# A hybrid retention and attention layer on one core: stores on another queue, loads in order, and late operands moved

## The chip, the cores and the metric

The kernel runs on one core of one Trainium2 chip. The metric is the device time of one execution in microseconds (us). TensorE does the matrix multiplications into PSUM (eight banks), VectorE (DVE in the profile) and ScalarE (ACT) the elementwise work, GpSimd (POOL) and SyncE (SP) issue transfers between the core's SBUF and HBM; ACT can issue them too.

## The reference

One layer over 512 tokens of 1024 channels, all in 32-bit floats:

```python
h = rms_norm(x, norm_mix)
rq, rk, rv, rg, cq, ckv, krope, gr, gm = split(h @ w_in)     # 4 retention heads, latents, two gates
ro = retention(rope(rq), rope(rk), rv)                       # heads of 256 and 512
ro = rms_norm(ro, ret_norm)
a_ret = (ro * silu(rg)) @ w_br
q, (k, v) = rms_norm(cq) @ w_uq, rms_norm(ckv) @ w_ukv       # 8 attention heads
a_mla = causal_attention(norm+rope(q), norm+rope(k), v) @ w_bm
x = x + (sigmoid(gr) * a_ret + sigmoid(gm) * a_mla) @ w_o
x = x + square(relu(rms_norm(x) @ w_up)) @ w_down
x = x + sigmoid(rms_norm(x) @ w_ple_gate) * (p @ w_ple)
```

## The kernel before

Everything is kept transposed, 128 channels by 512 tokens to a tile. Each 32-bit operand is split into a high part in TensorE's 32-bit format and the rest (`split`, lines 303 to 313), and each product is three multiplications (`mm3`). Weights come as chunks from one stream: `prepare` (lines 221 to 248) issues a chunk's load into one of 6 raw tiles (NRAW), `load_chunk` makes the high part on ACT and the rest on VectorE. The retention's v and gate and the MLP's second weight use a seven-product scheme on 2 by 2 blocks, in the order 1, 7, 2, 6, 5, 4, 3. There some weights are sums of blocks: SP loads one block and POOL adds another to it while loading (`accum_op`, line 227). Some operands are sums too: product 7 takes the difference of two token halves of the first four residual tiles, and products 6, 5 and 3 similar sums.

The work is written as a list of steps (`step(key, function, arguments)`), run in order by `run_steps`. A step with a key uses that chunk of weights; its loop prepares and converts chunks shortly ahead (AHEAD, PREP). Matrix multiplications keep the order in which they are written. The other engines' instructions are placed by a scheduler, which works with times of its own and can put an instruction in another place than it is written; `tc.keep_in_program_order` pins one behind the one written before it on its engine.

Tiles: `T(...)` takes one of NDYN = 45 tiles of the pool `dyn`, `K(...)` one of NKEEP = 16 of the pool `keep`. An instruction that needs a tile waits until one is free. The attention outputs (`mos`) hold all 16 keep tiles until the last product with `w_bm`.

The order of the stages, in which the change moves things:

- **Start.** Eight tiles of x (`x0` to `x7`) and eight chunks `a1` are loaded on SP; from them come the key/value latent (`pA`), then the query latent (`pcq`). `gn` (gains) is loaded from ACT, `cst` and `posi` from POOL.
- **Attention.** For each of 8 heads: `scores`, then other work while the softmax is made, `transposes` of the probabilities (`pt`), and in the next head's time `attend` (`mo`). `kq_head` projects two heads ahead; `pair_sums`, `pair_stats` (`st`, `hr`) and `head_factor` (`pbk`, `kf`) make the normalising factors of the next pair of heads, `rotary_stats` (`sqr`, from `sa`) those of four heads' rotary part. Between them stand fillers, `fill`: halves of the gate product `gm` and of head 0's `rq`, `rk` and the first `gr`, each 12 multiplications of 512 columns.
- **bm.** Eight products `branch_m`: each loads the gate that was put aside in HBM by `aside`, multiplies it by the product and puts it aside again (`am`). After each, `norm_x` loads one tile of x again (`xr`), scales it and splits it (`xn`). After all eight, `x_operands` makes the sums for products 7, 6, 5, 3 in keep tiles (`s70h` and so on).
- **Retention.** For each of 4 heads: `rq`, `rk`; for heads 0 and 2 the seven products `rv` of two heads; the branch products `br` of the head before; gate products `rg`, scores `rs`, `ret_attend` (`ro`), `ret_stats` (root `ro`, line 330), `ret_factor` (broadcast `pbo`, then four multiplications), `ret_gated` (gate, then the split `rog`). The branch outputs of head 0 are put aside, those of heads 1 and 2 added to them by POOL.
- **Gate, output, MLP, embedding.** Not touched by the diff.

The part of the list for the odd heads of attention:

```python
            if more:
                if h == 3:
                    step(None, rotary_stats, 1)
                step(None, pair_sums, p + 1)
                step(("v", p + 1), value_pair, p + 1)
                step(None, pair_stats, p + 1)
            else:
                fill(1)
            step(None, attend, h - 1)
            fill(1)
            step(None, transposes, h)
            if more:
                step(None, head_factor, h + 1)
                step(None, head_factor, h + 2)
            fill(1)
```

Of the kernel before, what the change touches and what calls it, by code (L numbers as in the profile page):

```python
# [151 lines left out]
def trunk_layer(ctx: ExitStack, tc: tile.TileContext, xT, pT, pos, gains, const, decay, wstream, outT):  # L152
# [68 lines left out]
    def prepare(key):  # L221

        if key[0] == "sw":
            _, blk, p, c = key

            def more(raw, kb, fb):
                nc.gpsimd.dma_start(raw, chunk(("w", blk, kb, fb, c)), accum_op=ALU.add)  # L227

            if p in (6, 4):
                return more(dw[blk, "t", c], *((0, 0) if p == 6 else (1, 0)))  # L230
            kb, fb = {1: (0, 0), 7: (0, 1), 2: (1, 0), 5: (0, 1), 3: (1, 1)}[p]
            nm = f"{blk[0]}{blk[1]}{p}{c}"
# [12 lines left out]
        nm = "_".join(str(x) for x in key)  # L245
        raw = wpool.tile([P, width], F32, tag="wraw", name="wr_" + nm, padded_shape=[P, 1024], bufs=NRAW)
        nc.sync.dma_start(raw, chunk(key))
        dw[key] = raw
# [23 lines left out]
    def run_steps():  # L272
        order = list(dict.fromkeys(k for k, _, _ in steps if k is not None))
        rank = {k: i for i, k in enumerate(order)}
        loaded = prepared = len(wt)
# [82 lines left out]
    nc.scalar.dma_start(gn, gains)  # L358
    posi = dyn.tile([P, S], I32, tag="t", name="posi")
    nc.gpsimd.dma_start(cst, const)  # L360
    nc.gpsimd.dma_start(posi, pos.partition_broadcast(P))
    xs, xg = [], []
    for k in range(8):
        t = T(f"x{k}")
        nc.sync.dma_start(t, xT[:, k])
# [335 lines left out]
    def x_operands():  # L701

        lo_, hi_ = slice(0, 256), slice(256, 512)
        for p, k0, cs in ((1, 0, lo_), (2, 4, lo_), (4, 4, hi_)):
            XS[p] = [(xn[k0 + k][0][:, cs], xn[k0 + k][1][:, cs]) for k in range(4)]

        def keep_split(p, c, t):
            hl = split(t, None, hi=K(f"s{p}{c}h", F32R), lo=K(f"s{p}{c}l", F32R))
            XS.setdefault(p, []).extend(cut(hl, kk * 256, 256) for kk in range(2))

        ts = [T(f"sx{c}") for c in range(2)]
        for p in (7, 6, 5, 3):
            for c in range(2):
                t = T(f"sy{c}") if p == 5 else ts[c]
                for kk in range(2):
                    k, o = 2 * c + kk, t[:, kk * 256:kk * 256 + 256]
                    if p == 7:
                        TT(o, xr[k][:, hi_], xr[k][:, lo_], op=ALU.subtract)
                    elif p == 6:
                        TT(o, xr[4 + k][:, hi_], o, op=ALU.subtract)  # L720
                    elif p == 5:
                        TT(o, xr[k][:, hi_], xr[4 + k][:, hi_], op=ALU.subtract)
                    else:
                        TT(o, xr[4 + k][:, lo_], o, op=ALU.subtract)
                keep_split(p, c, t)
# [96 lines left out]
    def ret_factor(h):  # L822
        r = R[h]["r"]
        R[h]["bc"] = bcast(B(f"pbo{h}"), lambda b: r[:, b:b + 1])
        for m in range(4):
            TT(R[h]["og"][m], R[h]["og"][m], R[h]["bc"], op=ALU.mult)

# [21 lines left out]
    def ret_gated(h):  # L849
        d = R[h]  # L850
        for m in range(4):
# [3 lines left out]
            d["rog"][m] = split(d["og"][m], f"rog{h}{m}")  # L855
# [270 lines left out]
    for h in range(MH):  # L1126
        p, more = h // 2, h + 2 < MH
        step(None, scores, h)
        if h % 2 == 0:
# [10 lines left out]
            if h == 2:  # L1140
                step(("qr", 1), query_rotary, 1)
            step(None, transposes, h)
            if h == 2:
                step(None, rotary_out, 1)
            fill(1)
        else:
            if more:
                if h == 3:
                    step(None, rotary_stats, 1)
                step(None, pair_sums, p + 1)  # L1150
                step(("v", p + 1), value_pair, p + 1)
                step(None, pair_stats, p + 1)
            else:
# [13 lines left out]
    fill(len(fillers))  # L1167
    step(None, mo_split, MH - 1)
    for n in range(8):
        step(("bm", n), branch_m, n)  # L1170
        step(None, norm_x, n)
    step(None, x_operands)
    for h in range(RH):
        for key in ("rq", "rk"):
            for n in range(2 if h else 0):
                step((key, h, n), ret_qk, h, key, n)
        left = [(("br", h - 1, k), branch_r, h - 1, k) for k in range(4 if h else 0)]
# [17 lines left out]
        step(None, ret_factor, h)  # L1195
# [3 lines left out]
    for n in range(EARLY, EARLY + 2):  # L1199
        step(("gr", n), gate_r, n)  # L1200
    for k in range(4):
# [113 lines left out]
```

## Time and profile before

| | |
|---|---|
| median of 3 runs | 1156.58 us (1153.46 to 1157.91) |
| profiled execution | 1155.4 us |
| its span | 1153.6 us |
| TensorE busy | 1110.3 us, 96% of the span |
| VectorE, ScalarE, GpSimd busy | 737.8, 537.0, 70.7 us |
| mean granted TensorE clock | 0.991 of full speed |
| moved by DMA | 173.33 MB, mean 150 GB/s |

A row of the profile's order of time reads: start and length in us from the span's start, engine (a q behind it: the engine's sequencer, which issues transfers), line of the kernel, operation, written tile <- read tiles, shape, count; in brackets the engine's idle time before it and what ended that. PE is TensorE's multiplication, PEld its weight load. A row of the chain of waits gives start, length and what ran. A row of the waits gives who waited <- for whom: total us, times, longest. Many rows have the line of a helper (172 for a multiplication, 265 to 269 for a weight's conversion, 308 to 312 for a split), so they are told apart by their tiles.

### The profile page before, as it was taken

The page shows a single profiled execution, that of the slowest core. Times are in us where ns is not written, and L with a number is a line of the kernel's source. Part 1 is how long each engine was busy: PE and PEld are TensorE (multiplying, and loading weights), DVE is VectorE, ACT ScalarE, POOL GpSimd, SP SyncE. Part 2 cuts the span into 40 slices and gives each one's busy share as a digit, 9 for nine tenths or more (in the row PEclk, how much of TensorE's full clock was granted, in tenths as well). Part 3 has the DMA queues.
Part 4 walks back from the last instruction along what each step waited for, and adds up shares of the span by engine and source line. Part 5 has one row for each costly group of instructions (what it writes and reads, how often), then busy time and mean ns, then how long its engine had stood idle before and what let it go on. Part 6 is the DMA issues. An engine that isn't in the chain of part 4 may idle for free.

```text
span 1153.6 us, 14652 instructions
## 1 busy us (share of the span) xinstructions
PE 1110.3 (96%) x5540; PEld 939.6 (81%) x5540; DVE 737.8 (64%) x1205; ACT 537.0 (47%) x762; POOL 70.7 (6%) x86
## 2 busy tenths in 40 slices
PE   6998989999699999999999999999999999999998
PEld 4887878888589788888989888888888888888877
DVE  5786666674775836745674765555567567568775
ACT  5555646553565344454534533433454344445542
POOL 0000000000110000121012000000100100101000
PEclk9998999999899999999999999999999999999999
DMA  6224121248785463598449443675756756747511
GB/s 224 76 79 131 55 76 62 74 157 248 178 224 138 137 186 119 131 208 239 132 130 194 146 182 109 192 243 168 151 163 196 155 159 179 169 143 192 155 36 73
DMA packets 59477, 173.33 MB, mean 150 GB/s; under 512 B 7088, under 2 KB 8368, under 8 KB 59152
## 3 DMA queue, kind: packets, MB, share of 16 engines
q1 hardware_dynamic: 47616, 134.24, 34.0%
q0 software_dynamic: 11648, 38.15, 19.1%
q8 instruction: 43, 0.70, 0.2%
q14 instruction: 26, 0.21, 0.1%
q10 hardware_dynamic: 144, 0.03, 0.0%
HBM read 155.61 MB, written 14.68 MB: 148 GB/s over the span
## 4 chain that ended last, share of the span: by engine, by line
PE 88%; DVE 5%; DMA 3%; ACT 2%; issue 2%; SPq 0%; POOL 0%; ACTq 0%; POOLq 0%; DVEq 0%
PE up L172 15%; PE dn L172 13%; PE br L172 8%; PE rv L172 5%; PE rg L172 5%; PE pg L172 4%; PE rq L172 4%; PE rk L172 4%; PE gr L172 4%; PE wo L172 3%; PE bm L172 3%; PE gm L172 3%; PE ro L172 3%; PE sc L172 2%; DMA wr_rg<-wstream 2%
## 5 line engine op out<-in xcount | busy, mean ns | idle before, releaser
L172 PE MATMUL dn<-wh_dn,cl 128*128 128x512 f32 x224 | 87.2, 389 | 0.0
L172 PE MATMUL dn<-wh_dn,ch 128*128 128x512 f32 x224 | 87.2, 389 | 0.0
L172 PE MATMUL dn<-wl_dn,ch 128*128 128x512 f32 x224 | 87.1, 389 | 0.0
L265 ACT ACTIVATE wh_dn<-wr_dn 128x1024 fp32r<-128x1024 f32 x32 | 34.0, 1062 | 75.5 <-PE up L172 54.3
L265 ACT ACTIVATE wh_up<-wr_up 128x1024 fp32r<-128x1024 f32 x32 | 34.0, 1061 | 57.7 <-PE up L172 29.3
L267 DVE TENSOR_TENSOR wl_dn<-wr_dn,wh_dn 128x1024 fp32r<-128x1024 f32 x32 | 39.1, 1221 | 27.4 <-ACT wh_dn L265 27.4
L267 DVE TENSOR_TENSOR wl_up<-wr_up,wh_up 128x1024 fp32r<-128x1024 f32 x32 | 39.1, 1223 | 18.5 <-ACT wh_up L265 18.1
L267 DVE TENSOR_TENSOR wl_rg<-wr_rg,wh_rg 128x1024 fp32r<-128x1024 f32 x20 | 24.5, 1225 | 40.5 <-ACT wh_rg L265 40.2
L172 PEld LDWEIGHTS dn<-wh_dn,ch 128*128 128x128 f32 x224 | 42.0, 188 | 8.8
L172 PEld LDWEIGHTS dn<-wh_dn,cl 128*128 128x128 f32 x224 | 42.0, 188 | 8.7
L172 PEld LDWEIGHTS dn<-wl_dn,ch 128*128 128x128 f32 x224 | 42.0, 188 | 8.6
L956 DVE SCALAR_TENSOR_TENSOR f<-up,bcx 128x512 f32<-128x512 f32 x32 | 20.6, 686 | 44.2 <-PE up L172 44.2
L265 ACT ACTIVATE wh_dn<-dr_dn 128x1024 fp32r<-128x1024 f32 x24 | 25.4, 1060 | 42.5 <-PE up L172 29.2
L267 DVE TENSOR_TENSOR wl_dn<-dr_dn,wh_dn 128x1024 fp32r<-128x1024 f32 x24 | 29.4, 1223 | 22.4 <-ACT wh_dn L265 22.4
L227 POOL DMA_DIRECT2D dr_dn<-wstream x24 | 21.7, 906 | 330.6 <-DVE rx L330 138.5
L265 ACT ACTIVATE wh_rg<-wr_rg 128x1024 fp32r<-128x1024 f32 x28 | 29.5, 1055 | 20.9 <-DMA wr_rg<-wstream 15.6
L265 ACT ACTIVATE wh_rv<-wr_rv 128x1024 fp32r<-128x1024 f32 x28 | 29.4, 1057 | 17.9 <-PE rv L172 6.3
L227 POOL DMA_DIRECT2D wr_rv<-wstream x16 | 13.8, 885 | 382.5 <-DMA wr_rv<-wstream 272.0
L863 ACT ACTIVATE rt<-br 128x512 f32<-128x512 f32 x24 | 14.3, 597 | 41.6 <-PE br L172 24.1
L1014 DVE TENSOR_TENSOR d<-d,dn 128x1024 f32<-128x1024 f32 x24 | 29.3, 1219 | 6.5 <-PE dn L172 6.5
L267 DVE TENSOR_TENSOR wl_br<-wr_br,wh_br 128x1024 fp32r<-128x1024 f32 x16 | 19.6, 1222 | 18.8 <-ACT wh_br L265 18.8
L265 ACT ACTIVATE wh_br<-wr_br 128x1024 fp32r<-128x1024 f32 x16 | 16.9, 1057 | 28.8 <-PE rk L172 17.8
(1889 smaller groups left out, 3620.8 us busy)
## 6 DMA issues: line engine op xcount, KB each, us to landing
wr_up<-wstream SPq DMA_DIRECT2D x32, 512.0 KB, 4.2
wr_dn<-wstream SPq DMA_DIRECT2D x32, 512.0 KB, 3.5
dr_dn<-wstream POOLq DMA_DIRECT2D x24, 512.0 KB, 8.4
wr_rv<-wstream SPq DMA_DIRECT2D x20, 512.0 KB, 4.5
wr_rg<-wstream SPq DMA_DIRECT2D x20, 512.0 KB, 5.2
wr_rv<-wstream POOLq DMA_DIRECT2D x16, 512.0 KB, 7.9
wr_rg<-wstream POOLq DMA_DIRECT2D x16, 512.0 KB, 6.2
wr_br<-wstream SPq DMA_DIRECT2D x16, 512.0 KB, 3.6
```

The source lines that it names most:

```text
L172: return tc.keep_in_program_order(nc.tensor.matmul(*a, **k))
L227: nc.gpsimd.dma_start(raw, chunk(("w", blk, kb, fb, c)), accum_op=ALU.add)
L265: ACT(hi, raw, AF.Copy, scale=sign)
L267: TT(lo, raw, hi.bitcast(F32), op=ALU.subtract)
L863: ACT(t, ps, AF.Copy)
L956: STT(u[:, i], ps[:, i], 0.0, V["bcx2"], op0=ALU.max, op1=ALU.mult)
L1014: TT(to, to, dps[p], op=ALU.add if sign > 0 else ALU.subtract)
```

## The change

- `aside` issues its 24 stores (8 `zm`, 8 `am`, 8 `ret`) from POOL and not from SP.
- Start: the loads of x0 to x7 go out from ACT in order, with `gn` behind x0; six chunks `a1` go out from SP in order, then `cst` and `posi`; the last two `a1` chunks keep that order too.
- `x_operands` becomes `x_operand(p)`, one step for each product. Product 7's operand is made after bm 2, its four parts in `dyn` tiles; the others after bm 7, as before in keep tiles. `norm_x` begins two tiles earlier, ahead of the last `mo_split`.
- `ret_factor` stands behind the next head's first `rq` product (for the last head, behind the first `gr` product), after the gating; it now makes the split too, the first two outputs of four in keep tiles.
- Attention: head 0's filler stands ahead of its transposes; for odd heads `attend` stands ahead of `rotary_stats` and `pair_stats`, and the last filler between transposes and head factors.

```diff
-        nc.sync.dma_start(raw, chunk(key))
+        tc.keep_in_program_order(nc.sync.dma_start(raw, chunk(key))) if key[0] == "a1" else nc.sync.dma_start(raw, chunk(key))
...
-        loaded = prepared = len(wt)
+        loaded, prepared = len(wt), len(dw)
...
         d = spill.tile([P, S], F32, tag=name, name=name + "d")
-        nc.sync.dma_start(d, t)
+        nc.gpsimd.dma_start(d, t)
...
-    nc.scalar.dma_start(gn, gains)
-    nc.gpsimd.dma_start(cst, const)
-    nc.gpsimd.dma_start(posi, pos.partition_broadcast(P))
     for k in range(8):
-        t = T(f"x{k}")
-        nc.sync.dma_start(t, xT[:, k])
-        xs.append(t)
-        if k < 3:
+        xs.append(T(f"x{k}"))
+        tc.keep_in_program_order(nc.scalar.dma_start(xs[k], xT[:, k]))
+        if k == 0:
+            tc.keep_in_program_order(nc.scalar.dma_start(gn, gains))
+        if k < 6:
             prepare(("a1", k))
-            load_chunk(("a1", k))
-            xg.append(split(t, f"xg{k}", g(G_MIX + k)))
+    tc.keep_in_program_order(nc.sync.dma_start(cst, const))
+    tc.keep_in_program_order(nc.sync.dma_start(posi, pos.partition_broadcast(P)))
+    for k in range(3):
+        load_chunk(("a1", k))
+        xg.append(split(xs[k], f"xg{k}", g(G_MIX + k)))
...
+            new = T if p == 7 else K
+            hl = split(t, None, hi=new(f"s{p}{c}h", F32R), lo=new(f"s{p}{c}l", F32R))
...
-            d["rog"][m] = split(d["og"][m], f"rog{h}{m}")
+    def ret_factor(h):
+        d, r = R[h], R[h]["r"]
+        bc = bcast(B(f"pbo{h}"), lambda b: r[:, b:b + 1])
+        for m in range(4):
+            TT(d["og"][m], d["og"][m], bc, op=ALU.mult)
+            new = K if m < 2 else T
+            d["rog"][m] = split(d["og"][m], None, hi=new(f"rog{h}{m}h", F32R), lo=new(f"rog{h}{m}l", F32R))
...
+            if h == 0:
+                fill(1)
             step(None, transposes, h)
...
-            fill(1)
+            if h:
+                fill(1)
         else:
+            if more:
+                step(None, pair_sums, p + 1)
+                step(("v", p + 1), value_pair, p + 1)
+            else:
+                fill(1)
+            step(None, attend, h - 1)
             if more:
                 if h == 3:
                     step(None, rotary_stats, 1)
-                step(None, pair_sums, p + 1)
-                step(("v", p + 1), value_pair, p + 1)
                 step(None, pair_stats, p + 1)
-            else:
-                fill(1)
-            step(None, attend, h - 1)
             fill(1)
             step(None, transposes, h)
+            fill(1)
             if more:
                 step(None, head_factor, h + 1)
                 step(None, head_factor, h + 2)
-            fill(1)
...
     fill(len(fillers))
+    step(None, norm_x, 0)
+    step(None, norm_x, 1)
     step(None, mo_split, MH - 1)
     for n in range(8):
         step(("bm", n), branch_m, n)
-        step(None, norm_x, n)
-    step(None, x_operands)
+        if n < 2:
+            step(None, norm_x, 2 + n)
+        elif n == 2:
+            step(None, x_operand, 7)
+        elif n < 7:
+            step(None, norm_x, n + 1)
+    for p in (1, 2, 6, 5, 4, 3):
+        step(None, x_operand, p)
...
                 step((key, h, n), ret_qk, h, key, n)
+                if (key, n) == ("rq", 0):
+                    step(None, ret_factor, h - 1)
...
-        step(None, ret_factor, h)
         step(None, ret_gated, h)
...
         step(("gr", n), gate_r, n)
+        if n == EARLY:
+            step(None, ret_factor, RH - 1)
```

More of the change, by code (lines that the diff above doesn't have):

```diff
@@ L699, in norm_x, with x_operand @@
         xn.append(split(t, f"xn{k}"))
-    def x_operands():
+    def x_operand(p):
         lo_, hi_ = slice(0, 256), slice(256, 512)
-        for p, k0, cs in ((1, 0, lo_), (2, 4, lo_), (4, 4, hi_)):
+        if p in (1, 2, 4):
+            k0, cs = {1: (0, lo_), 2: (4, lo_), 4: (4, hi_)}[p]
             XS[p] = [(xn[k0 + k][0][:, cs], xn[k0 + k][1][:, cs]) for k in range(4)]
[L707 to L722, printed above, removed]
-                    else:
-                        TT(o, xr[4 + k][:, lo_], o, op=ALU.subtract)
-                keep_split(p, c, t)
+            return
+        if p == 7:
+            V["sx"] = [T(f"sx{c}") for c in range(2)]
+        XS[p] = []
+        for c in range(2):
+            t = T(f"sy{c}") if p == 5 else V["sx"][c]
+            for kk in range(2):
+                k, o = 2 * c + kk, t[:, kk * 256:kk * 256 + 256]
+                if p == 7:
+                    TT(o, xr[k][:, hi_], xr[k][:, lo_], op=ALU.subtract)
+                elif p == 6:
+                    TT(o, xr[4 + k][:, hi_], o, op=ALU.subtract)
+                elif p == 5:
+                    TT(o, xr[k][:, hi_], xr[4 + k][:, hi_], op=ALU.subtract)
+                else:
+                    TT(o, xr[4 + k][:, lo_], o, op=ALU.subtract)
+            new = T if p == 7 else K
+            hl = split(t, None, hi=new(f"s{p}{c}h", F32R), lo=new(f"s{p}{c}l", F32R))
+            XS[p].extend(cut(hl, kk * 256, 256) for kk in range(2))
     CHAIN = {1: "a", 6: "a", 5: "a", 3: "a", 7: "c", 4: "c", 2: "b"}
@@ L820, in ret_stats @@
         R[h]["r"], _ = mean_rsqrt(f"ro{h}", st, RV)
[L822 to L826, printed above, removed]
     rgps = {}
```

2 lines of the change are left out of this document (1 added, 1 removed).

## The prediction

> **What bounds the kernel now.** I read the shares of busy time first, then the chain that ended last, then TensorE's own waits, and last the instructions in order of time around the largest of those waits.
>
> ```profile
> span 1153.6 us, 14652 instructions
> PE 1110.3 (96%) x5540; PEld 939.6 (81%) x5540; DVE 737.8 (64%) x1205; ACT 537.0 (47%) x762; POOL 70.7 (6%) x86
> ...
> PE 88%; DVE 5%; DMA 3%; ACT 2%; issue 2%; SPq 0%; POOL 0%; ACTq 0%; POOLq 0%; DVEq 0%
> ```
>
> TensorE is busy for 96% of the span and holds 88% of the chain. Nothing in the diff adds or removes a matrix multiplication, so what can be won is in TensorE's idle time, 1153.6 - 1110.3 = 43 us, and in the multiplications that run slowly after an idle stretch. The waits of TensorE, longest first (total, times, longest):
>
> ```profile
> PE rv L172 <- DVE s70l L309: 8.4, 1, 8.4
> PE pbo L172 <- DVE ro L330: 6.6, 4, 1.7
> PE pA L172 <- ACT xg0h L311: 4.8, 1, 4.8
> PE pbk L172 <- DVE hr L599: 3.8, 3, 1.5
> PE pt0a L172 <- ACT q2h L311: 3.5, 1, 3.5
> PE pA L172 <- ACT xg1h L311: 2.9, 1, 2.9
> PE sqr L172 <- DVE sa L557: 2.1, 1, 2.1
> PE st L172 <- ACT sums L584: 1.3, 1, 1.3
> ```
>
> Each row is a place that the diff moves: product 7's operand (s70l), the head factor of the retention (pbo), the start (pA), the key factors (pbk), the first transposes (pt0a), the statistics (sqr, st). No row names a weight's DMA: the queues wait a great deal, but TensorE does not wait for them. So the work on the queues is worth little by itself, and I price the four places in turn. All prices are set against the profiled execution's own 1155.4 us, which is 1.2 us under the median of the runs, 1156.58.
>
> **Part 1: the start.** Order of time, the first 31 us:
>
> ```profile
> 0.73 0.41 ACTq L358 DMA_DIRECT2D gn<-gains  x1
> 1.18 1.28 ACT L265 ACT_TABLE_LOAD   x1 [1.18 <-PEq L1308]
> 1.64 3.67 SPq L247 DMA_DIRECT2D wr_a<-wstream  x6
> 4.07 0.72 ACT L311 ACTIVATE xg0h<-x,gn 128x512 fp32r<-128x512 f32 x1 [0.36 <-DMA x<-xT]
> 4.84 0.80 PE L172 MATMUL pA<-xg0h,wl_a 128*128 128x512 f32 x1 [4.84 <-ACT xg0h L311]
> 5.36 0.59 SPq L365 DMA_DIRECT2D x<-xT  x1
> 11.36 0.72 ACT L311 ACTIVATE xg1h<-x,gn 128x512 fp32r<-128x512 f32 x1 [1.17 <-DMA x<-xT]
> 12.13 0.66 PE L172 MATMUL pA<-xg1h,wl_a 128*128 128x512 f32 x1 [2.90 <-ACT xg1h L311]
> 28.45 0.39 PE L172 MATMUL pA<-xg7h,wl_a 128*128 128x512 f32 x1
> 30.49 0.39 PE L172 MATMUL pcq<-xg0h,wl_cq 128*128 128x512 f32 x1
> ```
>
> Six weight loads stand on SP ahead of x1, which is issued at 5.36 and is only there at 11.36. A step is nine multiplications, 30.49 - 28.45 = 2.04 us at pace, so eight steps are 16.3 us; they take 30.49 - 4.84 = 25.65 us, 9.3 us too many. The change puts x0 to x7 in order on ACT's queue beside the weights on SP, so x1 lands soon after x0, and the wait of 2.9 us and the second slow stretch behind it go. It costs something too: nine DMA issues (gn and eight x) now stand on ACT ahead of its first conversion. By the SP row an issue in a row takes 3.67/6 = 0.61 us, so ACT is free at about 0.73 + 9 x 0.61 = 6.2 us; the table load of 1.28 us then follows them in place of running beside the first load, and a weight conversion (three quarters of xg0h's columns, about 0.5) and xg0h (0.72) bring the first multiplication to about 8.7 us, 3.9 later than now. After it only one slow stretch of about 2.6 us over the pace is left: 8.7 + 16.3 + 2.6 = 27.6 against 30.49, a gain of 2.9; I take 3. Ends: if the two queues' issues hold each other up to twice 0.61 us, ACT is free 5.5 us later and 2.6 us are lost; if the issues take 0.41 like gn's, 1.8 us more are won, 4.7 in all.
>
> The Trainium skill (DMA: Bandwidth & Descriptors, section Issuing engines are not separate DMA queues) says that DMAs started from several engines run on the same DMA engines, and that a second queue saves only issue time. By that alone the start would gain nothing, and the sum below would be 1135. The rows above say that it was the order on one queue that kept x1 back, so I keep the 3 us.
>
> Moving cst and posi behind the weights on SP I cost at nothing: TensorE first reads cst behind the latent products. The mask's two copies on ACT read it too; if they stand early in ACT's order, they wait for it there, which I leave inside the ends.
>
> **Part 2: attention.** The first transposes, and the chain of small VectorE steps behind one pair's factors:
>
> ```profile
> 104.30 0.82 DVE L641 TENSOR_SCALAR p<-p,rs 128x384 f32<-128x384 f32 x2
> 105.26 1.09 PE L172 MATMUL pt0a<-cst,p 128*128 128x128 f32 x4 [3.50 <-ACT q2h L311]
> 108.28 0.63 PE L172 MATMUL gm<-xg0h,wh_gm 128*128 128x512 f32 x1
> 121.28 0.17 DVE L595 TENSOR_TENSOR ha<-st,f 128x16 f32<-128x16 f32 x1
> 127.38 0.17 DVE L599 TENSOR_TENSOR hr<-hr,f 128x16 f32<-128x16 f32 x1
> ```
>
> TensorE stands still for 3.5 us until the softmax rows are scaled (104.30 + 0.82), then takes 0.63 for a multiplication that takes 0.39 in the rows of part 1. A filler of 12 multiplications (12 x 0.227 = 2.7 us) now stands in that gap: 2.7 of the 3.5 us go, and with a gap of 0.8 us no slow stretch should follow (some nine multiplications, each about 0.2 late, near 2.0). Behind it, scores of head 1 come 2.7 us sooner against transposes and projections whose PSUM banks are not yet emptied; I set 0.5 against it. Gain 4.2.
>
> For the odd heads, attend moves ahead of the pair's statistics and a filler moves between the transposes and the factor's broadcast. The VectorE chain takes 127.38 - 121.28 + 0.17 = 6.3 us. After the change two fillers and ten transposes (2.7 + 1.4 + 2.7 = 6.8, with four transposes at the 0.62 of part 4's row) lie between the statistics and the broadcast, so of the three pbk waits (3.8) I leave 0.5. The waits on sa (2.1) and on sums (1.3) have attend's 12 multiplications ahead of them now, some 2 us, and go. Gain 3.3 + 2.1 + 1.3 = 6.7, less 0.4 for what else may come late: 6.3. Part 2: 10.5, ends 6 (the banks cost 2 to 3, half of pbk stays) and 13.
>
> **Part 3: product 7's operand.** The last residual tile is asked for late, and the operand's sums stand behind it:
>
> ```profile
> 296.87 0.43 SPq L696 DMA_DIRECT2D xr<-xT  x1
> 304.69 0.75 DVE L697 SCALAR_TENSOR_TENSOR xr<-xr,gn,rbc 128x512 f32<-128x512 f32 x1 [1.94 <-DMA xr<-xT]
> 307.09 1.43 DVE L718 TENSOR_TENSOR sx<-xr 128x256 f32<-128x256 f32 x4
> 309.51 0.80 PE L172 MATMUL rv<-wh_rv,s70l 128*128 128x512 f32 x1 [8.41 <-DVE s70l L309]
> 310.10 0.63 PE L172 MATMUL rv<-wl_rv,s70h 128*128 128x512 f32 x1
> 310.53 0.63 PE L172 MATMUL rv<-wh_rv,s70h 128*128 128x512 f32 x1
> ```
>
> ```profile
> 301.00:306.00 5.00, 0.10 (x1) 0.00 (x0) 2.00 (x3) 2.10 (x3) 1.36 (x2) 0.99 1.07 235
> ```
>
> The sums need only xr0 to xr3, but VectorE did them behind xr7, which came at 304.69; and their results lay in the 16 keep tiles, all held by the attention outputs until the last bm product. With tiles of their own, and sums made when bm 2 is issued, they are ready more than 20 us before TensorE gets there. The 8.4 us go, and so does the slow stretch: seven steps of 0.43 in place of 0.23, with the first at 0.59, together 1.6. That is 10.0.
>
> What is late next: the weights. The last row is the stretch in which TensorE stood still (columns: length, busy time of PE, PEld, DVE, ACT, POOL, then granted clock, DMA share, GB/s): the DMA engines were full (1.07) while TensorE waited, so part of the stall hid transfers that the products after it need. Taken away, 10 us less lie between the bm products and product 3. For it: two xr loads are moved ahead of the bm products, SP no longer waits for each gated product before it issues the next load, and VectorE has made product 7's sums already. I set 3 us against it, ends 0 and 8. Part 3: 7.
>
> Stores: the 24 store issues move from SP to POOL. On SP nothing that TensorE waits for stood behind them (no weight row above), so nothing is gained there directly. On POOL they stand between the accumulating weight loads. One of POOL's accumulating stores, of head 2's branch:
>
> ```profile
> 602.59 0.87 POOL L867 DMA_DIRECT2D ret0d<-rt  x1 [1.71 <-ACT rt L863]
> ```
>
> That is the mix already: it takes 0.87 us and waits on ACT, and TensorE's waits have no row for the gate products behind it. A store that waits on its producer delays an accumulating load by one branch step at most. Cost 0.5, ends 0 and 3.
>
> The Trainium skill (DMA: Bandwidth & Descriptors, section SWDGE vs HWDGE vs iDMA) gives plain copies to SP and ACT, since GpSimd writes its descriptors in software and can be locked out by VectorE. By that rule the stores would be dearer; here 0.87 us of issue on an engine busy 6% of the span is no bound, so I leave the sum.
>
> **Part 4: head factors.**
>
> ```profile
> 379.42 0.62 PE L172 MATMUL pbo<-cst,ro 128*128 128x128 f32 x4 [1.63 <-DVE ro L330]
> ```
>
> Four times TensorE waits about 1.65 us (6.6) for the reciprocal root. Moved behind the next head's first rq product (24 x 0.227 = 5.4 us), the broadcast finds it ready. The factor, the split and the branch product now follow later: for heads 0 to 2 three or more products (16 us) still lie between, enough for 4 multiplications and 4 splits (8 x 0.68 = 5.4 us of VectorE). For head 3 only one gate product (5.4 us) lies between, where there were two; I set 0.6. Gain 6.0, ends 3 and 6.6.
>
> **Tiles.** Product 7's four operand tiles now live in the dyn pool through all four heads, and four of the eight factored outputs leave it for the keep pool, but only while a branch product needs them. In head 0, ahead of the scores, the pool holds 2 tables, 1 early gate, 16 residual tiles, 8 of rq and rk, 16 of v and 2 of z: 45 of NDYN = 45. With four more, the last v split and both z copies wait until the scores free the rq and rk tiles; the same in head 2. Behind the scores two gate products (up to 360.56) cover two ACT copies and a split:
>
> ```profile
> 350.92 3.88 PE rs L172 x24
> ...
> 360.56 7.71 PE ro L172 x48
> ```
>
> ```profile
> 356.50 0.68 DVE L798 TENSOR_TENSOR s<-rs,dec 128x512 f32<-128x512 f32 x1
> ```
>
> The masked scores already start 1.7 us after the scores' end (354.8) and are needed 4 us later, when attend begins, so 1 to 2 us more are late once each; then og and its square are short of a tile until head 0's v is free. I take 1.5 us for each of the two heads, 3 in all, ends 0 and 10.
>
> **Sum.** 3 + 10.5 + 7 - 0.5 + 6 - 3 = 23.0; 1155.4 - 23.0 = 1132.4. The median stood 1.2 above the profiled execution, and I say 1133.
>
> **Rivals.**
> A. All covers hold: the start gains 4.7, attention 13, part 3 10, part 4 6.6, no tile is short: 34, so 1121. For it: every wait above has a named cause that the edit takes away. Against it: full DMA engines and a full pool.
> B. The tiles and the DMAs take more: 8 in part 3, 10 for the tiles, the rest as forecast: 3 + 10.5 + 2 - 0.5 + 6 - 10 = 11, so 1144. For it: the count of 45 and the DMA share of 1.07.
> C. No change: waits only change place. VectorE's chains (6.3 us behind the statistics, the root) end as late as before, since each reorder shifts its own start too; then only part 3 is left, its 7 less the tiles' 3, and the start at its loss of 2.6: 1.4 won, 1154. Against it: the factor's broadcast gets 5.4 us of cover for a wait of 1.65 whatever starts when.
> D. Slower, by the dyn pool alone: if the missing tiles hold up TensorE for a whole attend product (7.7 us in that row) in each of the four heads, with a slow stretch of 1.6 behind each, that is 37 us against 26 won without the tiles' price: 1166. It decides from 6.5 us a head on. Against it: heads 1 and 3 hold only 8 v tiles and have room.
>
> **How the numbers follow.** Chances: the forecast (within 6 us of 1133) 0.51, A 0.17, B 0.17, C 0.08, D 0.07. The range of 8 in 10 leaves out D and most of C and the best of A: 1121 to 1150. About 0.5% (5.8 us) can be told from no change by these runs. Faster takes the forecast, A and B and a little of C: 0.86; the same 0.07; slower 0.07.
>
> **What would show it.** Right: in TensorE's waits the rows of s70l and pbo gone, pt0a under 1 us, pbk under 1 us in all; first multiplication near 8.7 us and the first cq product near 27.6; granted clock near 1.0 in the bm to rv stretch. Wrong: rows of rv or rg that wait for wl_rv or a DMA (part 3), rows of so, ro or rg waiting for ACT or VectorE copies (tiles), or a start beyond 30 us. What would break the prediction is an order on ACT or VectorE that the edits change far from where they stand, since unpinned instructions are placed by a scheduler.

## The result, and the profile after

| | before | after |
|---|---|---|
| median | 1155.76 us (1153.46 to 1157.91, 4 runs) | 1139.95 us (1137.74 to 1143.38, 4 runs) |
| profiled execution, its span | 1155.4, 1153.6 us | 1137.74, 1136.0 us |
| TensorE busy | 1110.3 us | 1103.0 us |
| mean granted clock | 0.991 | 0.998 |

The ratio is 0.9866 (95% interval 0.9833 to 0.99). Between the medians 15.8 us are won, between the two spans 17.6; the forecast was 23.0 and 1133, with a range of 1121 to 1150.

The shares of busy time and of the chain after the change:

```profile
span 1136.0 us, 14670 instructions
PE 1103.0 (97%) x5540; PEld 935.0 (82%) x5540; DVE 736.8 (65%) x1205; ACT 535.7 (47%) x762; POOL 83.0 (7%) x108
...
PE 89%; DMA 4%; DVE 3%; ACT 2%; issue 1%; SPq 0%; POOL 0%; ACTq 0%; POOLq 0%
```

The chain has passed a little from VectorE (5 to 3%) to DMA (3 to 4%). TensorE's waits (total, times, longest):

```profile
PE pA L172 <- ACT xg0h L311: 11.4, 1, 11.4
PE rv L172 <- DVE wl_rv L267: 6.8, 2, 5.3
PE mo L172 <- DVE zm L674: 2.9, 1, 2.9
PE rv L172 <- ACT wh_rv L265: 1.4, 1, 1.4
...
PE pbk L172 <- DVE hr L600: 0.8, 1, 0.8
PE br L172 <- ACT rog32h L308: 0.8, 1, 0.8
...
PE pt0a L172 <- DVE p L642: 0.7, 1, 0.7
...
PE br L172 <- DVE rog32l L309: 0.4, 1, 0.4
```

The rows of s70l, pbo, xg1h, q2h, sa and sums are gone. In their place stand a start of 11.4 us, and 8.2 us of rv products that wait for weights, where such rows came to 1.4 us before. Where the time went is best read from the start of the same multiplication in both traces; the gains of the stages between such marks add up to the whole:

| stretch | forecast | measured |
|---|---|---|
| to the first cq product (30.49, now 29.90) | 3.0 | 0.6 |
| attention, to the first bm product (251.98, now 242.04) | 10.5 | 9.3 |
| bm products to the first rg product (93.0 long, now 92.6) | 7.0, less 0.5 for the stores | 0.4 |
| head factors (1.8, 1.8, 1.8 and 0.1) | 6.0 | 5.5 |
| rv products of head 2 | none | 1.4 |
| tiles in heads 0 and 2 | -3.0 | no wait of their own |
| tail | none | 0.4 |
| sum | 23.0 | 17.6 |

The start. The loads on the two queues and what follows them, then the wait of SP's fifth weight load and the length of ACT's eight x issues (least, median and most in ns):

```profile
0.74 1.81 SPq L247 DMA_DIRECT2D wr_a<-wstream  x4
1.66 0.94 ACTq L362 DMA_DIRECT2D x<-xT  x2
4.39 0.33 ACTq L362 DMA_DIRECT2D x<-xT  x1
6.86 1.94 ACTq L362 DMA_DIRECT2D x<-xT  x4
8.82 1.28 ACT L265 ACT_TABLE_LOAD   x1 [8.82 <-DMA x<-xT]
11.38 0.77 PE L172 MATMUL pA<-xg0h,wl_a 128*128 128x512 f32 x1 [11.38 <-ACT xg0h L311]
```

```profile
SPq L247 <- DMA x<-xT: 2.0, 1, 2.0
L362 ACTq DMA_DIRECT2D x<-xT x8: 334/424/454, 0.7 to 8.4; - x8
```

An issue on ACT took 0.33 to 0.45 us, about as long as that of the gains before (0.41). But eight loads (four weights, the gains, x0 to x2) were out on the two queues by 2.6 us, and the next issue went out only at 4.39. From the ninth on, an issue on either queue goes out only when the load eight places ahead of it has landed: in the trace the loads take turns on eight semaphores. ACT stood some 4 us in such waits (from 2.60 to 4.39 and from 4.72 to 6.86). It was free at 8.8 us and TensorE began at 11.4, where 6.2 and 8.7 were forecast. The eight steps then ran in 18.5 us with one slow stretch, as forecast (18.9).

Product 7 and what came behind it, first the loads and the order on ACT and VectorE, then the stretches (length, busy time of PE, PEld, DVE, ACT, POOL, granted clock, DMA share, GB/s):

```profile
285.37 0.39 SPq L682 DMA_DIRECT2D gb<-zm6d  x1
...
291.68 0.39 PE L172 MATMUL rv<-wh_rv,s70l 128*128 128x512 f32 x1
293.67 0.63 ACT L684 ACTIVATE gb<-gb 128x512 f32<-128x512 f32 x1 [4.83 <-DMA gb<-zm6d]
294.20 1.04 ACT L265 ACTIVATE wh_rv<-wr_rv 128x1024 fp32r<-128x1024 f32 x1
295.30 0.51 PE L172 MATMUL rv<-wh_rv,s71l 128*128 128x512 f32 x1 [1.42 <-ACT wh_rv L265]
301.40 0.60 ACT L737 ACTIVATE cv<-rv 128x512 f32<-128x512 f32 x1 [3.59 <-DMA am6d<-gb]
303.93 1.05 ACT L265 ACTIVATE wh_rv<-wr_rv 128x1024 fp32r<-128x1024 f32 x1
305.62 0.80 PE L172 MATMUL rv<-wl_rv,xn4h 128*128 128x512 f32 x1 [5.28 <-DVE wl_rv L267]
```

```profile
293.00:300.00 7.00, 4.06 (x17) 2.74 (x16) 5.64 (x11) 3.67 (x5) 1.44 (x2) 1.00 1.04 246
300.00:306.00 6.00, 0.72 (x3) 0.38 (x2) 3.94 (x7) 4.60 (x9) 0.58 (x1) 0.97 0.57 124
306.00:312.00 6.00, 6.00 (x21) 4.80 (x21) 4.01 (x5) 3.00 (x4) 0.86 (x1) 0.75 0.67 197
```

s70l no longer holds TensorE: at the second rv product's start 8.6 us were won (18.5 us ahead of before, where the first was 9.9 ahead). By the fourth product only 10.4 were left: 8.2 gone again, and with them the 1.6 that the missing slow stretch was to bring. ACT stands for 4.8 us at the gate's sigmoid, whose reload was issued as late as 285.37 and took 8.2 us to land (4.2 for the one before it), and for 3.6 us at cv, whose tile is still being stored (am6d). The convert of the next weight stands behind each of them in ACT's order, and TensorE behind the convert. That both waits hang on tiles of the common pool was the reading to test.

### The profile page after: what moved, and what is told of

Read it like the earlier page. It is cut to its first block, busy times and chain, and to the rows that moved or that the text cites. A ratio compares the mean times of both kernels' runs of the same rounds, so it can differ in the third digit from the quotient of the medians.

```text
span 1136.0 us, 14670 instructions
## 1 busy us (share of the span) xinstructions
PE 1103.0 (97%) x5540; PEld 935.0 (82%) x5540; DVE 736.8 (65%) x1205; ACT 535.7 (47%) x762; POOL 83.0 (7%) x108
## 4 chain that ended last, share of the span: by engine, by line
PE 89%; DMA 4%; DVE 3%; ACT 2%; issue 1%; SPq 0%; POOL 0%; ACTq 0%; POOLq 0%
PE up L172 15%; PE dn L172 13%; PE br L172 8%; PE rg L172 7%; PE rv L172 6%; PE pg L172 4%; PE rq L172 4%; PE rk L172 4%; PE wo L172 3%; PE gr L172 3%; PE gm L172 3%; PE ro L172 3%; PE sc L172 2%; PE pA L172 2%; PE pcq L172 1%; PE bm L172 1%
## 5 line engine op out<-in xcount | busy, mean ns | idle before, releaser
L265 ACT ACTIVATE wh_rv<-wr_rv 128x1024 fp32r<-128x1024 f32 x28 | 29.6, 1057 | 19.2 <-PE rv L172 11.9
L267 DVE TENSOR_TENSOR wl_rv<-wr_rv,wh_rv 128x1024 fp32r<-128x1024 f32 x20 | 24.5, 1224 | 12.2 <-ACT wh_rv L265 12.2
L639 ACT ACTIVATE p<-p,ng,hr 128x128 f32<-128x128 f32 (+3 forms) x32 | 20.6, 645 | 15.8 <-DVE ng L637 15.8
```

What stands on the lines that cost most here:

```text
L265: ACT(hi, raw, AF.Copy, scale=sign)
L267: TT(lo, raw, hi.bitcast(F32), op=ALU.subtract)
L639: ACT(cols[b], cols[b], AF.Exp, bias=ng[:, b:b + 1], scale=d["rq"][:, b], accum_out=sums[:, b:b + 1])
```

## The experiments

Two theories for these 10 us. *Tiles and order*: the gate's eight buffers share the pool of 45 with everything else, so their reloads and stores fall into the first rv products, and ACT's order turns each into a late weight. *Transfers or the stores' queue*: the weights themselves are late, since more has to land in less time, or since stores now stand between the accumulating loads on POOL. The length from the first bm to the first rg product is the measure: it holds the same multiplications in every kernel here, and in two profiles of one kernel (all covers, below) it took 81.9 and 82.4 us. A total says less where a kernel ran once: the changed kernel's own four runs lie 5.6 us apart.

### The stores back on SP

```diff
-        nc.gpsimd.dma_start(d, t)
+        nc.sync.dma_start(d, t)
```

> The changed kernel with its 24 stores back on SP, nothing else. Open: why products rv wait 8.2 us for weight conversions (6.8 on VectorE's part, 1.4 on ACT's) after the change. Theory: ACT's copy of product 1 or 7 was given the tile that the gated product am6 still holds; that store is late because POOL issues it behind accumulating loads, so from SP it lands sooner: the 5.3 us wait falls below 2 and the rv stretch is 4 to 6 us shorter, time 1132 to 1135. Rival 1, full DMA engines: the same bytes in the same stretch, the waits stay within 2 us of 8.2, time 1137 to 1140. Rival 2, SP's queue: a store that waits holds the next loads back, and the waits grow past 11 us, time above 1141.

Measured: 1145.54 us, slower than the changed kernel's 1137.74 (1143.38 in its slowest run). The rv products wait 7.1 us for weights in place of 8.2, and the bm to rg stretch took 94.4 us (92.6), so the weights' waits are not the work of POOL's queue. Another 4.4 us went in head 0's attend, of which 2.3 are one new wait, and the rest is a clock that drops behind it (0.78 and 0.79 from 354 to 362 us); head 2's attend lost 1.5:

```profile
PE ro L172 <- ACT ath L308: 3.4, 2, 2.3
```

### The old start

The changed kernel with the start of before: gains first on ACT's queue, x on SP behind the weights, cst and posi on POOL's.

> The changed kernel with the loads of the start as before the change. Theory: the new start is worth 0.6 us (first cq product at 29.90 against 30.49), because ACT's eight x issues push its first conversion to 10.1 us and eat what the order wins; so first cq product near 30.5 and all later stages 0.6 later. Rival: the start also shifts something later (the order in which tiles are handed on), then a later stage moves by more than 1 us.

Measured: 1143.79 us. The first multiplication began at 5.18, the first cq product at 33.90, 4.0 later than after and 3.4 later than before, though it is before's start. The difference is mostly the clock behind the wait for xg1h (3.4 us here). It stood at 0.51 and 0.63 in these two stretches, and at 0.57 and 1.00 in the kernel before:

```profile
12.00:16.00 4.00, 3.27 (x7) 2.31 (x8) 2.07 (x4) 2.44 (x4) 0.00 (x0) 0.51 0.77 242
16.00:20.00 4.00, 4.00 (x13) 2.97 (x11) 1.80 (x3) 1.04 (x2) 0.00 (x0) 0.63 0.93 341
```

So the new start is worth 0.6 or 4 us, by how long the old one stays slow. In all profiles here the old start reaches the first cq product at 30.49, 31.02, 32.32 and 33.90 us, and the new one in six at 28.92 to 30.27: 2.3 us apart in the mean. The rival came true as well: the attends of heads 0 and 2 took 1.3 and 1.5 us more than in the changed kernel, with waits for ath. They do so in several kernels here, whatever was changed.

### x on both queues

```diff
-        tc.keep_in_program_order(nc.scalar.dma_start(xs[k], xT[:, k]))
+        tc.keep_in_program_order((nc.scalar if k < 2 else nc.sync).dma_start(xs[k], xT[:, k]))
```

> The changed kernel with only x0, the gains and x1 issued from ACT, and x2 to x7 from SP between the weight chunks, in order. Theory (ACT is held by its own issues): three issues end near 2 us, first multiplication near 5, first cq product at 24 to 26, time 4 to 6 us under the changed kernel's. Rival (the bytes are the bound: DMA engines full from 2 to 12 us): first multiplication near 5 but later steps wait for x, first cq product at 28 or later, gain under 2.

Measured: 1141.17 us in all, but the start is what it tests. With three issues on ACT the first multiplication began at 8.20 and the first cq product at 27.14, 2.8 sooner with the same bytes: ACT standing behind its own issues was what made the start late. The theory's 5 and 24 to 26 were missed, since ACT now converts three weights ahead of xg0h, the last of them landed at 7.0. Later 3.4 us were lost at head 2's attend, and the most at the wait of mo, which is 2.9 us here as in the changed kernel. There the clock stayed at 1.00; here it fell, and the stretch from head 3's to head 4's scores took 26.4 us in place of 22.2:

```profile
151.00:155.00 4.00, 1.12 (x3) 0.94 (x4) 3.53 (x11) 2.21 (x4) 0.54 (x1) 0.76 0.33 82
...
159.00:163.00 4.00, 4.00 (x13) 3.33 (x13) 2.77 (x18) 0.47 (x1) 0.00 (x0) 0.50 0.53 121
```

The Trainium skill (TensorE: Matmul & The Clock Gate, section What's actually happening) puts the clock's choice on the activity in windows of some 3.4 us that run freely. The same wait of 2.9 us with and without a drop agrees with windows that fall differently.

### The gate's buffers in tiles of their own

```diff
-        t = T(f"gb{n}")
+        t = dyn.tile([P, S], F32, tag="qp", name=f"gb{n}", bufs=6)
```

The six qp tiles held the attention's queries and lie idle by now.

> The changed kernel with the eight gb tiles of the bm products in the six tiles that attention's rotary queries (qp) no longer use, and not in the dyn pool. Theory (a tile handed on while its store is out): ACT's copy in the rv stretch no longer waits for the am6 store (3.6 us of ACT's idle time), the 5.3 us wait of TensorE falls below 2, time 1131 to 1134. Rival (full DMA engines, weights late): the wait only changes its name, rv waits stay above 6 us, time 1136 to 1140.

Measured: 1133.91 us. No rv product waits any more, and the bm to rg stretch is 82.0 us: 10.7 won on the changed kernel, 11.1 on before. That decides for tiles and order against the stores' queue, which is the same. The bytes are the same too, but not their time: zm6d's reload goes out at 252.18 and not at 285.37, and lands in 3.8 us and not in 8.2. Some 6 us were lost again at z and ath in head 0 (waits of 1.4 and 2.3 us, and a clock of 0.67 behind them).

### z in the same tiles

The same six tiles also take the retention's z (three lines, `T(...)` becoming the call above).

> On the previous run (the gate's buffers in the six tiles of the attention's queries) the retention's sixteen z tiles go into those six too, so that the common pool of 45 has more room in the retention. Theory, tiles: the waits rg <- z (1.4 us) and ro <- ath (3.1 us with a clock drop of about 3 us behind them) of that run come from tiles of the common pool that free late; they go, the span is 1126 to 1129 us (1132.1 less 3 to 6). Rival, order on ScalarE: its convert of a late-landed weight stands ahead of z and ath, the tiles do not matter; the two waits stay within 1 us of what they were and the span stays at 1131 to 1134 us.

Measured: 1130.07 us, span 1128.3. The waits of rg for z and of ro for ath are gone but for 0.2 us, as the theory said; head 0's attend (first ro product to the broadcast) took 23.5 us in place of 27.1. The gate's last reload is now issued at 259.04, 27 us sooner than in the changed kernel, and TensorE stays busy where it stood still:

```profile
259.04 0.37 SPq L685 DMA_DIRECT2D gb<-zm7d  x1
...
293.00:300.00 7.00, 7.00 (x33) 5.76 (x32) 5.61 (x8) 4.98 (x9) 0.87 (x1) 1.00 1.04 184
300.00:306.00 6.00, 6.00 (x28) 4.99 (x27) 1.93 (x2) 2.62 (x3) 0.86 (x1) 1.00 0.89 248
```

The DMA share in 293 to 300 is 1.04 in both kernels, so full DMA engines alone do not make TensorE wait. They are not cleared altogether: without the reloads 184 GB/s moved there in place of 246, and the late reload's 8.2 us to land were part of ACT's wait.

### The operand part alone, on the kernel before

norm_x and the operand sums as in the change, with all else as before; the rog halves of m 0 and 1 move to the keep pool, since the counts of tiles hang together.

> The kernel before with one part of the change alone: norm_x spread between the output products and product 7's operand ahead of the other sums (the tiles for the rog halves of m 0 and 1 are moved with it, since the counts of tiles are tied). Stores stay on SyncE's queue, start, attention and head factors are as before. Theory, weights: the 10 us of product 7's wait for its operand turn into waits of the rv products for late weights plus slow clock, wherever the stores are; the second to fifth rv products lose 8 to 10 us again and the gain on the kernel before is 0 to 2 us (1154 to 1156 of span about 1153.7 in the profile). Rival, stores or the other parts: the loss behind product 7 belongs to the stores on GpSimd's queue or to the earlier arrival of this stage; alone this part keeps 7 to 10 us (1146 to 1149).

Measured: 1159.25 us beside 1159.41 of before. Against the mark of the first bm product the second rv product came 8.6 us sooner, and by the fourth 11.9 had gone again: the stretch to rg took 96.4 us in place of 93.0. So this part by itself loses 3 us there, with the stores on SP and no other edit. (The totals say little: the kernel before ran at 1153 to 1159 us.) Counted from the first bm product, zm6d's reload goes out at 37.4 us in the kernel before, at 43.3 in the changed kernel, at 46.1 here and at 10.5 with tiles of its own. The late gate stands in its trace in the same place:

```profile
PE rv L172 <- DVE wl_rv L267: 7.8, 2, 6.7
...
302.31 0.63 ACT L683 ACTIVATE gb<-gb 128x512 f32<-128x512 f32 x1 [4.90 <-DMA gb<-zm6d]
302.85 1.04 ACT L265 ACTIVATE wh_rv<-wr_rv 128x1024 fp32r<-128x1024 f32 x1
```

### The operand part with the tiles

The same, with gb and z in the qp tiles.

> The kernel before with the operand part alone, as in the run of that part, and with the gate's buffers and the retention's z in the six tiles of the attention's queries. Theory, tiles and order on ScalarE: the operand part alone lost its gain because the gate's reloads wait for tiles of the common pool, come in during the retention's first products, and the gate's operation on ScalarE stands ahead of the converts of weights; with the reloads early nothing of that is left, the rv products from the second on keep 8 to 11 us on the kernel before, and the span is 1142 to 1147 us (1153.6 less 8.6 and less up to 3). Rival, transfers: the weights themselves land late because stores and reloads share the DMA engines with them, and the changed kernel was helped by its stores' queue; the rv products still wait 4 us and more and the span is 1149 to 1156.

Measured: 1153.05 us, span 1151.2. That is above the theory's 1142 to 1147 and inside the rival's 1149 to 1156, and the rv products still wait 4.1 us for wl_rv, as the rival had it. But the stretch to rg took 86.7 us: 9.7 of the operand part's 11.9 lost us come back, and 6.3 are won on before, where the theory asked for 8 to 11. On before, another 2.1 us were lost ahead of the bm products (partly a slow clock behind the old wait for sa) and 1.8 in the attends of heads 0 and 2. So tiles are most of it and not all. The 4.1 us that are left fit the stores, which stand on SP here: the rv weights' loads go out behind them as in the last run below, where the same wait is 4.1 us too and is gone with the stores on POOL. No run of this kernel with its stores on POOL settles it.

### The tiles, with the stores on SP

> The changed kernel with the gate's buffers and z in the queries' tiles, and the stores back on SyncE's queue. Theory: the stores' queue mattered in the changed kernel only by the time at which the gate's tiles came free; with those out of the common pool the queue is worth less than 1.5 us, the span is 1126 to 1131 us (1128.3 with the stores on GpSimd's queue, where an idle dropped the clock once). Rival: stores on SyncE's queue hold up the weight loads behind them by 1 to 3 us each wherever the tiles are; the rv or ro products wait 3 us and more and the span is 1132 to 1137.

Measured: 1138.97 us, span 1137.2, against 1128.3 with the stores on POOL. The rv products hardly wait (0.9; the stretch is 83.1), but ro waits 3.4 us for ath in heads 0 and 2, and the attends take 3.4 and 4.3 us more with the clock's drop. ACT stands at a weight of rg with ath behind it:

```profile
345.00 1.06 ACT L268 ACTIVATE wh_rg<-wr_rg 128x1024 fp32r<-128x1024 f32 x1 [1.82 <-DMA wr_rg<-wstream]
345.96 0.40 ACT L311 ACTIVATE ath<-s 128x256 fp32r<-128x256 f32 x1
```

The theory (under 1.5 us) failed: with the gate's tiles out of the pool the stores' queue still makes a difference, though not at the gate.

### The two new waits covered

```diff
+            if h:
+                fill(1)
             if h == 2:
                 step(None, rotary_out, 1)
-            if h:
-                fill(1)
...
-    for n in range(EARLY, EARLY + 2):
+    for n in range(EARLY, EARLY + 3):
```

> The changed kernel with the two waits that are new in it covered: at head 2 the filler product stands ahead of rotary_out's seven VectorE instructions, and three instead of two gate products stand ahead of the last head's output products. Theory, covers: the wait of mo for zm (2.9 us) and those of br for bcx, rog32h and rog32l (2.4 us together) go, and the time is 3 to 6 us below the changed kernel beside it or, against 1137.7, 1132 to 1135. Rival, renaming: the same VectorE queue is late for the next product, a wait of another name takes 2 to 3 us in the same place and the time stays within 1.5 us of 1137.7 (up to 1143 where an idle drops the clock).

Measured: 1136.73 us. The wait of mo went, but 1.3 us at pt3a and 0.8 at mx took part of its place: the stretch of that pair is 1.4 us shorter, not 2.9. Behind head 3's factor 1.8 us were won and 0.7 lost at the tail. So about half of each theory. Another 2.4 us were lost at ath in heads 0 and 2, so that the total hardly moved.

### All covers together

Gate and z in the qp tiles, x on both queues with the first three weights' and x's converts in a written order, both new waits covered.

> All of them together: two x blocks on ScalarE's queue and six on SyncE's with the first converts in a written order, the gate's buffers and z in the queries' tiles, the filler ahead of rotary_out, three gate products ahead of the last output products. Theory: the gains add: start 2.8, attention 2.9, gate's tiles 4 to 8, end 1.5 to 2.4, so 1122 to 1127 us. Rival, late weights: each stage that comes earlier meets weights that were only just in time, a third to a half is given back, 1127 to 1132 us.

> The version with all the covers together, timed: 1120.68 in one run so far. Theory: it repeats within 0.3% since no idle of more than 2 us is left that could drop the clock: median 1119 to 1123, ratio to the kernel before 0.967 to 0.972. Rival: the start and the waits at p and mx (1.3 and 0.8 us) still drop the clock in some runs, median 1123 to 1127, ratio 0.971 to 0.976.

Measured: 1120.68 us in one run, then a median of 1122.18 (1120.23 to 1127.95, 5 runs), ratio to before 0.9727 (0.9703 to 0.9751). In the first run's profile the first cq product starts at 25.23, the stretch to rg takes 81.9 us, and these are the waits of over 1 us that are left:

```profile
PE pA L172 <- ACT xg0h L316: 6.1, 1, 6.1
PE pt3a L172 <- DVE p L649: 1.3, 1, 1.3
PE pg L172 <- ACT bcx L951: 1.2, 1, 1.2
```

The gains add to 17 us on the changed kernel's profile, more than the theory's sum: 4.7 in the start, 1.4 at head 2's filler, 10.7 in the stretch to rg, 1.8 behind head 3's factor, less 1.5 elsewhere. It is faster than both kernels. The runs do not repeat within 0.3%: they lie 0.7% apart, with the median in the theory's range and the ratio in the rival's.

### All covers, with the stores on SP

> The version with all the covers together, with its stores back on SyncE's queue: the price of the queue alone, timed, against 1122.18 of the same version with the stores on GpSimd's queue. Theory: what two single runs showed is the queue's price; with stores on SyncE's queue the ro products of heads 0 and 2 wait 1.5 to 2 us each for ath and the clock drops behind them, median 1127 to 1132, 5 to 9 us more. Rival: those waits were one placement of the instructions on ScalarE and SyncE among several; in another version they are under 1 us and the median lies within 3 us, 1120 to 1125.

Measured: median 1127.51 (1125.23 to 1131.04, 5 runs), ratio 0.9741 (0.9728 to 0.9754). The medians stand 5.3 us apart, as the theory had it, but the two ratios' intervals overlap, so the times alone don't settle it. The two profiles say where, but they are the slowest of these five runs and the fastest of the other five: the stretch to rg takes 88.8 us (82.4 with the stores on POOL), with 4.7 us of rv waits for weights (none), and head 2's attend 3.4 us more. The theory had looked for the loss at the ro products alone. The first bm product starts at 235.6 here and at 235.2 there. With the stores on SP, rows in order of time and last a row of SP's own waits from 258 to 290 us:

```profile
265.97 0.75 DVE L705 SCALAR_TENSOR_TENSOR xr<-xr,gn,rbc 128x512 f32<-128x512 f32 x1 [5.47 <-DMA xr<-xT]
...
267.35 0.33 SPq L361 DMA_DIRECT2D am4d<-gb  x1
267.77 0.38 SPq L704 DMA_DIRECT2D xr<-xT  x1
268.82 0.33 SPq L240 DMA_DIRECT2D wr_rv<-wstream  x1
...
SPq L361 <- DVE sx L726: 19.6, 4, 7.3
```

With the stores on POOL:

```profile
265.05 0.33 SPq L240 DMA_DIRECT2D wr_rv<-wstream  x1
265.43 0.49 SPq L704 DMA_DIRECT2D xr<-xT  x1
```

VectorE stands 5.5 us for an xr tile and makes the store's product only behind it; four stores hold SP for 19.6 us in all, up to 7.3 each (the row names sx, VectorE's next instruction). The next xr and weight loads go out behind the store, so the weight at 268.82 is 3.8 us later than its like with the stores on POOL (265.05), and the two behind it are 3.9 and 3.8 later.

## Why the prediction was right in sign and 7 us too hopeful

**Start** (3, was 0.6). The order held: x1 came in time and one slow stretch was left. What failed is the time at which ACT is free, 6.2 us forecast and 8.8 measured. The 0.61 us for an issue came from a row of the kernel before that runs from the first of six issues to the end of the last. Taken apart, five of them took 0.47 us each, and the sixth waited for a weight's conversion:

```profile
1.64 2.34 SPq L247 DMA_DIRECT2D wr_a<-wstream  x5
4.32 0.99 SPq L247 DMA_DIRECT2D wr_a<-wstream  x1
```

So issues were priced too dear, and a wait was put at nothing: that an issue on ACT can stand until an earlier load has landed, some 4 us in all. The result lies between the forecast and the end given for queues that hold each other up. The split start shows it: its three issues on ACT are among the first eight loads, ACT is free at 2.1 us, and 2.8 us come back. The 0.6 is partly chance, too, as the old start varies by 3.4 us. The rule of the Trainium skill (DMA: Bandwidth & Descriptors, section Issuing engines are not separate DMA queues), set against the 3 us in the prediction, would have given nothing. This pair's 0.6 is near it; the split start, 3.4 us sooner than the kernel before, is not.

**Attention** (10.5, was 9.3). pt0a fell from 3.5 to 0.7, the rows of sa and sums went, pbk kept 0.8. What was missed is a wait that the reorder made: attend for head 2 now asks early for zm, and VectorE works off rotary_out's seven operations first. 2.9 us went there:

```profile
148.89 0.75 DVE L552 SCALAR_TENSOR_TENSOR o<-pqa,gn,tmc 128x512 f32<-128x512 f32 x1 [1.53 <-PE sc L172]
...
155.85 0.69 DVE L674 TENSOR_TENSOR zm<-gm,rbc 128x512 f32<-128x512 f32 x1
```

**Product 7's operand** (7, was 0.4). This is the step that failed. The 10.0 us fit: with the gate's own tiles the stretch wins 11.1 on before, with stores on POOL, and 6.3 with the operand part alone and stores on SP. The 3 set against them should have been near 10. The prediction said that weights would be late next, and so they were, but not by full DMA engines alone: it looked at the share of 1.07 in the stretch and not at what stood ahead of the weights' converts on ACT. Giving the gate tiles of its own, with the same bytes to move, wins 10.7 us back on the changed kernel and 9.7 on the operand part.

**Stores** (cost 0.5; the runs point to a gain). The reason was that no row showed a wait behind a store on SP (two rows of rv for wl_rv, 0.8 and 0.6 us, stood below those listed). That may hold only while TensorE waits 8.4 us for s70l in that same place; no run moves the stores alone in the kernel before. Three pairs of kernels differ in this queue alone: 5.3 us between timed medians with overlapping intervals, 7.4 and 8.9 in single profiles. The loss is not in one place: the stretch to rg has 6.4, 1.8 and 0.3 us of it, and most of the rest is at ath, where kernels with stores on POOL lost up to 4.4 us too.

**Head factors** (6.0, was 5.5). The waits of 1.65 went and took a slow restart with them, 1.8 each. For head 3 the cover of one gate product was too thin: 0.6 was set against it and 1.8 lost, at rog32h and rog32l and in the slow multiplications behind. A third gate product ahead took that away.

**Tiles** (-3 for v, z and og in heads 0 and 2). The changed kernel's trace has no such wait in head 0 and under 0.1 us in head 2. The pool was short, as counted, but the count was made for the wrong place: it bit at the gate's reloads, ahead of the rv products, where two prices of the sum (weights and tiles) are one. Part 3's 3 and the tiles' 3 together, 6, stood against some 10 measured. That the total came no lower is partly luck: the tiles' 3 were not needed in the heads, and 1.8 us came from places that had no price (the rv products of head 2, also won by the operand part alone, and the tail).

The median of 1139.95 lies inside the range of 1121 to 1150 and outside the 6 us around 1133 that the prediction called the forecast. Rival B (1144) is nearer, 4 us away. Its 8 in part 3 was close; its 10 for the tiles, meant for the retention's heads, did not come there.

## What to carry to other kernels

A long wait hides the shorter ones in its place. Before you book it as a gain, list for the products right behind it what each engine's queue still has to do at that time: here a reload and a store, both for lack of a tile, stood ahead of the weights' converts on ACT. If a pool is counted full, ask first which of its users has a transfer in flight, and give that one tiles of its own. Look also at what waits on the queue that feeds the weights: here a store that waited for its producer held the next loads up by nearly 4 us. And take a row that merges several issues apart before you divide it by their number, since the waits between them are in it.

## What the runs showed of the hardware beside that

Issuing a transfer is short, but an engine can stand behind its own issues. In the changed start an x issue took 0.33 to 0.45 us on ACT, and ACT stood some 4 us between them until earlier loads, of either queue, had landed; it did no other work before 8.8 us. Whether the program's eight semaphores alone set that limit, no run here shows.

A wait of TensorE can cost more than itself. 2.9 us at mo cost nothing further in the changed kernel, with the clock at 1.00, and some 4 us more in the kernel with the split start, with the clock at 0.50; 1.6 us at ath in head 0 were followed by a clock of 0.75 and 0.82 in the run of the tiles with stores on SP:

```profile
346.00:350.00 4.00, 3.51 (x15) 3.19 (x16) 3.60 (x5) 3.38 (x7) 0.00 (x0) 0.75 0.22 55
350.00:354.00 4.00, 4.00 (x22) 3.58 (x21) 1.15 (x3) 2.35 (x4) 0.00 (x0) 0.82 0.65 209
```

The Trainium skill (TensorE: Matmul & The Clock Gate, section Why this matters for your kernels) asks for no idle gap over some 3 us. Here shorter ones were enough in some runs.
